# A projection's PSUM bank, one sum instead of two, and softmax reciprocals on GpSimd in a decoder layer

## The chip, the cores and the metric

The kernel runs on one core of a Trainium2 chip. The metric is the device time of one execution in microseconds, as the median of several runs. TensorE is called PE below (its weight loads PEld), VectorE is DVE, ScalarE is ACT, GpSimd is POOL, and SP is the queue that issues most DMAs.

## The reference, cut to what matters

One decoder layer on 512 tokens of width 1024, all in float32:

```python
h = rmsnorm(x, g_mix_pre)
z = h @ w_in                       # columns of four head groups
ya = short_conv_mixer(a_in, a_c, a_b, conv_w)
yb = pool_mixer(pv, pool_w, pool_scale)
yc = dsa_mixer(...)                # 4 heads, each query keeps its 128 best-scored keys
yd = moba_mixer(...)               # 4 heads, causal softmax
mix = concat([ya, yb, yc, yd]) @ w_out
x = x + rmsnorm(mix, g_mix_post)
f = swiglu(rmsnorm(x, g_ffn_pre), w_gate_up, w_down)
x = x + rmsnorm(f, g_ffn_post)
x = x + sigmoid(rmsnorm(x, g_ple) @ w_ple_gate) * (p @ w_ple_proj)
```

The softmax of both attention mixers divides every row of exponentials by its sum. `rmsnorm` scales each token by the reciprocal root of the mean of its squares.

## The kernel before, in words

**Layout.** Activations stand with the features on the 128 partitions and the 512 tokens along the free dimension, so a vector of 1024 features is eight tiles. Every operand of a projection is split into a high and a low part, and a product is three matmuls (`mm3`, L188 to L190): high by high, high by low, low by high. Weights arrive in pieces in the order of `PLAN`; `get` (L180) sees to it that the piece two places ahead is split, the high part by ACT (L169), the low part by DVE or POOL (L173), whichever `lo_engine` names.

**Order.** PE's instructions stand in the order in which they are written. The other engines' order in the attention stage is planned when the kernel is built, from the builder's own durations; inside `with tc.manual_schedule()`, as in `boundary`, all engines keep the written order. All engines take their instructions in order. `later` and `tick` put work off by a number of PE steps.

**PSUM.** Eight banks in three rings: `pmm` (four), `pss` (two), `ptt` (two). A new tile of a ring takes the bank of the oldest one, and waits until that has been read.

**Attention.** The values' projection (L551 to L559) fills all four `pmm` banks. ACT and then DVE take each of the four out (L564, L565). Then `attend` (L654) runs 32 units, a head and a block of 128 queries each: first 16 of `moba`, then 16 of `dsa`. Each unit is `logits` (two matmuls into `pss`, DVE's bias and row maximum at L606, ACT's exponential with its row sum in `st[:, 1:2]` at L608), `weights` (the reciprocal of that sum at L612, a multiplication by it on ACT at L613) and, three units later, `transpose` (PE at L627 into `ptt`, ACT at L630, DVE at L631); `values` closes a head. Between these PE runs steps of `fill`: the remaining projections, of which `keep("pv0")` is the first. `helper` (L569) gives POOL the low parts, bias sums and some elementwise work in units below 20, and DVE the same from unit 20 on. The rounds of the top-128 search (L508, L509) are DVE work that goes in between.

**Boundaries.** Two times, after `w_out` and after `w_down`, `boundary` (L846) closes one norm and starts the next projection. Its last operand tile comes from `post(pt, 7, ...)`: ACT's square of it is `sq7`; the squares of the first seven tiles are already summed in `sums`. `Rms.add` multiplies four 128-column blocks by a column of ones, which gives each token's sum on the partitions; `Rms.sums` does this for `sums` and then for `sq7` into the same columns, then DVE scales (L254) and POOL takes the power of -1/2 (L255). `spread` transposes the four columns back into a full tile in a `ptt` bank (L260). While that chain runs, PE does steps of the small `ple` product (24 matmuls in eight steps) through `go`; ACT takes its four results out (L822). After the spread DVE multiplies and adds (L865, L870), ACT and DVE split (L873, L877), and the first matmul at L908 needs tile 0 of that. Of the eight steps, three are ahead of the spread and five behind it.

Of the kernel before, what the change touches and what calls it, by code (L numbers as in the profile page):

```python
# [9 lines left out]
F32 = mybir.dt.float32  # L10
F32R = mybir.dt.float32r
AF = mybir.ActivationFunctionType
OP = mybir.AluOpType
# [3 lines left out]
P = 128  # L17
# [5 lines left out]
NT = T // P  # L23
# [82 lines left out]
def tile_trunk(ctx: ExitStack, tc: tile.TileContext, xT, pT, sm, relx, wts, outT):  # L106
    nc = tc.nc
    G = ctx.enter_context(tc.tile_pool(name="glob", bufs=1))
# [4 lines left out]
    def pmm():  # L113
        return ps.tile([P, T], F32, tag="mm", bufs=4, name="pmm")

    def pss():
        return ps.tile([P, T], F32, tag="s", bufs=2, name="pss")

    def ptt():
        return ps.tile([P, T], F32, tag="tt", bufs=2, name="ptt")  # L120
# [7 lines left out]
    def tick():  # L128
        clock[0] += 1
        due = [p for p in put_off if p[0] <= clock[0]]  # L130
        put_off[:] = [p for p in put_off if p[0] > clock[0]]
        for _, fn, args in due:
            fn(*args)
# [61 lines left out]
    def single(name, act, pt, ks, start=True, stop=True, cw=P):  # L195

        w = get(name)
        for i, k in enumerate(ks):
            mm3(pt[:cw], w, act[k], (slice(None), slice(i * cw, (i + 1) * cw)), ALL,
                start and i == 0, stop and i == len(ks) - 1)  # L200
            if i < len(ks) - 1:
                yield
# [24 lines left out]
    smt = G.tile([P, SMW], F32, name="smt")  # L227
    ones = G.tile([P, 1], F32, name="ones")
    nc.vector.memset(ones, 1.0)
    mhalf = G.tile([P, NT], F32, name="mhalf")  # L230
    nc.vector.memset(mhalf, -0.5)

# [6 lines left out]
    class Rms:  # L239

        def add(self, sq, first, last):
            if first:
                self.pt = pss()
            for j in range(NT):
                nc.tensor.matmul(self.pt[:, j:j + 1], sq[:, j * P:(j + 1) * P], ones, start=first and j == 0,
                                 stop=last and j == NT - 1, skip_group_check=True)

        def sums(self, sq, first=True):  # L250
            self.add(sq, first, True)
            pt = self.pt
            self.r4 = G.tile([P, NT], F32, tag="r4", bufs=2, name="r4")
            nc.vector.tensor_scalar(self.r4, pt[:, :NT], 1.0 / D, 1e-6, OP.mult, OP.add)  # L254
            nc.gpsimd.tensor_tensor(self.r4, self.r4, mhalf, OP.pow)  # L255
# [19 lines left out]
    with tc.tile_pool(name="mix", bufs=1) as M:  # L275
        def tmp(shape=(P, T), name="tmp", dt=F32):
            return M.tile(list(shape), dt, tag="tmp", bufs=8, name=name)
# [298 lines left out]
        class Attn:  # L576
# [32 lines left out]

            def weights(self, it):  # L610
                st, pr = self.st.pop(it), self.pr[it]
                nc.vector.reciprocal(st[:, 2:3], st[:, 1:2])  # L612
                nc.scalar.activation(pr, pr, AF.Copy, scale=st[:, 2:3])  # L613

            def transpose(self, it):
# [69 lines left out]
        plain = {}  # L685

        def keep(name):
            pt = pmm()
            yield from single(name, h, pt, K8)
            z = plain[name] = tmp(name=name)  # L690
            nc.vector.tensor_tensor(z, pt, r1.rb, OP.mult)
            if name[:2] == "pv":
                pool_sums(int(name[2]))
            if name[:3] == "a_b":
                conv_group(int(name[3]))
            yield

        def pool_sums(m):
            v = plain.pop(f"pv{m}")
            s, w = v, 1  # L700
            for lv in range(2 * m + 2):
                rows = slice(64, P) if lv == 2 * m + 1 else slice(0, P)
                t = tmp(name="ws")
                nc.gpsimd.tensor_tensor(t[rows, w:], s[rows, w:], s[rows, :T - w], OP.add)
                nc.gpsimd.tensor_copy(t[rows, :w], s[rows, :w])
                if lv < 2 * m + 1:
                    s, w = t, 2 * w
            fa = _SM["fac"][0] + 16 * m
            for rows, u in ((slice(0, 64), s), (slice(64, P), t)):
                nc.gpsimd.tensor_tensor(u[rows, :16], u[rows, :16], smt[rows, fa:fa + 16], OP.mult)  # L710
                later(16, nc.vector.scalar_tensor_tensor, t[rows], u[rows], col("invw", m)[rows], v[rows], OP.mult,
                      OP.subtract)
            later(17, pool_split, m, t)
# [17 lines left out]
        def conv_group(m):  # L731
            a, c, b = (plain.pop(f"{n}{m}") for n in ("a_in", "a_c", "a_b"))
            eng = helper()
            eng.tensor_tensor(a, a, c, OP.mult)
            eng.tensor_scalar(c, a, col("conv", 3 * m + 2), 1.0, OP.mult, OP.mult)

            def taps():
                for s in (1, 2):
                    nc.vector.scalar_tensor_tensor(c[:, s:], a[:, :T - s], col("conv", 3 * m + 2 - s), c[:, s:],
                                                   OP.mult, OP.add)  # L740
                eng.tensor_tensor(c, c, b, OP.mult)
                y[m] = (yslot("yh"), yslot("yl"))
                later(3, split, y[m][0], y[m][1], c, 1)
            later(4, taps)
# [80 lines left out]
        for n in range(3, 8):  # L825
            pt = pt3 if n == 3 else pmm()
# [16 lines left out]
            if n < 7:  # L843
                post(pt, n, "g_mix_post", mg[n], ss, tmp)

        def boundary(sums, sq7, fill, x, add, gname, hdst, xdst, sqt, name):  # L846


            def go(n):
                for _ in range(n):  # L850
                    if next(fill, 0) == 0:
                        return
                    tick()
            r = Rms()
            r.add(sums, True, False)
            r.sums(sq7, False)
            low2 = convert_high(conv[0])
            go(3)
            r.spread(False)
            xs, hs, sqs = [], [], []  # L860
            ss = G.tile([P, T], F32, tag="ss", bufs=1, name="ss")

            def mul(k):
                if k < KD:
                    nc.vector.tensor_tensor(add[k], add[k], r.rb, OP.mult)  # L865

            def plus(k):
                if k < KD:
                    xn = xdst(k)
                    nc.vector.tensor_tensor(xn, add[k], x[k], OP.add)  # L870
                    xs.append(xn)
                    hs.append((hdst("hhi"), hdst("hlo")))
                    nc.scalar.activation(hs[k][0], xn, AF.Copy, scale=col(gname, k))  # L873

            def low(k):
                if k < KD:
                    nc.vector.scalar_tensor_tensor(hs[k][1], xs[k], col(gname, k), hs[k][0].bitcast(F32),  # L877
                                                   OP.mult, OP.subtract)

            def square(k):  # L880
                sqs.append(ss if k == 0 else sqt(name="sq"))
                nc.scalar.activation(sqs[k], xs[k], AF.Square)

            mul(0)
            plus(0)
            go(1)
            mul(1)
            plus(1)
            low(0)
            mul(2)  # L890
            go(8)
            pts = [pmm() for _ in range(4)]
            for k in K8:
                if k % 2 == 0:
                    w = wparts.pop(f"{name}{k // 2}")
                    send(conv[0] + RAW)
                plus(k + 2)
                low(k + 1)
                mul(k + 3)
                if 0 < k < 5:  # L900
                    square(k - 1)
                if k % 2 == 0 and k > 0:
                    low2 = convert_high(conv[0])
                if k == 0 or k % 2 and k > 1:
                    low2()
                c = [slice(((k % 2) * 4 + n) * P, ((k % 2) * 4 + n + 1) * P) for n in range(4)]
                for n in range(4):
                    nc.tensor.matmul(pts[n], w[0][:, c[n]], hs[k][0], start=k == 0, stop=False)  # L908
                for n in range(4):
                    nc.tensor.matmul(pts[n], w[1][:, c[n]], hs[k][0], start=False, stop=False)  # L910
                for n in range(4):
                    nc.tensor.matmul(pts[n], w[0][:, c[n]], hs[k][1], start=False, stop=k == KD - 1)  # L912
                tick()

            for k in range(1, KD):
                if k + 3 < KD:
                    square(k + 3)
                nc.vector.tensor_tensor(ss, ss, sqs[k], OP.add)
            return xs, hs, pts, ss

        with tc.manual_schedule():
            sq7 = post(pt, 7, "g_mix_post", mg[7], ss, tmp)
# [4 lines left out]
    with tc.tile_pool(name="ffn", bufs=1) as F:  # L927
# [60 lines left out]
        for n in range(KD):  # L988
            pt = pmm()
# [15 lines left out]
        with tc.manual_schedule():  # L1005
            sq7 = post(pt, 7, "g_ffn_post", fg[7], ss, ftmp)
# [22 lines left out]
        for c in (slice(0, 256), slice(256, T)):  # L1029
            pt = pmm()  # L1030
# [70 lines left out]
```

## Time and profile before

| what | value |
|---|---|
| median of 3 runs | 662.59 us (662.24 to 662.73) |
| profiled execution | 662.23 us, span 660.4 us |
| PE busy | 649.7 us, 98% of the span |
| DVE, ACT, POOL busy | 413.5, 283.0, 74.2 us |
| granted TensorE clock | 0.998 of full speed |

Busy time of PE counts pipelined matmuls; for PE, the idle stretches in front of an instruction, with the instruction that ended them, say more than the share. The timeline's columns are: start in us, duration in us, engine, line, operation, output<-inputs, count, and in brackets the idle time before it and what ended it.

### The profile page before, as it was taken

The page shows a single profiled execution, that of the slowest core. Times are in us where ns is not written, and L with a number is a line of the kernel's source. Part 1 is how long each engine was busy: PE and PEld are TensorE (multiplying, and loading weights), DVE is VectorE, ACT ScalarE, POOL GpSimd, SP SyncE. Part 2 cuts the span into 40 slices and gives each one's busy share as a digit, 9 for nine tenths or more (in the row PEclk, how much of TensorE's full clock was granted, in tenths as well). Part 3 has the DMA queues.
Part 4 walks back from the last instruction along what each step waited for, and adds up shares of the span by engine and source line. Part 5 has one row for each costly group of instructions (what it writes and reads, how often), then busy time and mean ns, then how long its engine had stood idle before and what let it go on. Part 6 is the DMA issues. An engine that isn't in the chain of part 4 may idle for free.

```text
span 660.4 us, 8002 instructions
## 1 busy us (share of the span) xinstructions
PE 649.7 (98%) x2993; PEld 533.5 (81%) x2993; DVE 413.5 (63%) x717; ACT 283.0 (43%) x464; POOL 74.2 (11%) x72
## 2 busy tenths in 40 slices
PE   8999999999999999999999999999999999999997
PEld 7887878888777888888888888888888888888886
DVE  6969999998984468665555555555532322243867
ACT  7655255756785555333232323323222322233542
POOL 1112457365021000000000000000000000000000
PEclk9999999999999999999999999999999999999999
DMA  8447522443435513333332332323233323242203
GB/s 311 148 167 229 148 84 94 113 118 89 112 105 202 151 53 96 93 99 95 96 96 95 96 96 97 95 96 96 87 120 104 103 92 107 87 128 65 80 16 127
DMA packets 24774, 74.16 MB, mean 112 GB/s; under 512 B 3522, under 2 KB 3906, under 8 KB 24736
## 3 DMA queue, kind: packets, MB, share of 16 engines
q1 hardware_dynamic: 22656, 67.78, 33.1%
q0 software_dynamic: 2080, 5.88, 2.5%
q8 instruction: 23, 0.38, 0.2%
q14 instruction: 15, 0.12, 0.1%
HBM read 67.20 MB, written 4.74 MB: 109 GB/s over the span
## 4 chain that ended last, share of the span: by engine, by line
PE 78%; DVE 14%; DMA 3%; ACT 2%; issue 2%; SPq 0%; DVEq 0%; ACTq 0%
PE pmm L188 10%; PE pmm L190 9%; PE pmm L189 9%; PE pss L190 7%; PE pss L188 7%; PE pss L189 7%; PE ptt L188 6%; PE ptt L190 6%; PE ptt L189 6%; DVE acc L509 3%; DVE m L508 3%; PE pmm L908 2%; PE pmm L912 2%; PE pmm L910 2%; PE pmm L325 2%
## 5 line engine op out<-in xcount | busy, mean ns | idle before, releaser
L169 ACT ACTIVATE whi<-raw 128x1024 fp32r<-128x1024 f32 (+2 forms) x111 | 113.8, 1025 | 245.0 <-PE pmm L189 82.6
L173 DVE TENSOR_TENSOR wlo<-raw,whi 128x1024 fp32r<-128x1024 f32 (+2 forms) x96 | 112.6, 1173 | 99.7 <-ACT whi L169 99.6
L188 PE MATMUL pss<-hhi,whi 128*128 128x512 f32 (+1 forms) x184 | 72.0, 391 | 0.0
L190 PE MATMUL pss<-hhi,wlo 128*128 128x512 f32 (+1 forms) x184 | 71.7, 390 | 0.0
L189 PE MATMUL pss<-hlo,whi 128*128 128x512 f32 (+1 forms) x184 | 71.6, 389 | 0.0
L188 PE MATMUL pmm<-gth,whi 128*128 128x512 f32 x176 | 69.3, 394 | 0.0
L190 PE MATMUL pmm<-gth,wlo 128*128 128x512 f32 x176 | 69.0, 392 | 0.0
L189 PE MATMUL pmm<-gtl,whi 128*128 128x512 f32 x176 | 68.3, 388 | 0.0
L188 PE MATMUL ptt<-hhi,whi 128*128 128x512 f32 x168 | 65.6, 390 | 0.0
L190 PE MATMUL ptt<-hhi,wlo 128*128 128x512 f32 x168 | 65.4, 389 | 0.0
L189 PE MATMUL ptt<-hlo,whi 128*128 128x512 f32 x168 | 65.4, 389 | 0.0
L188 PE MATMUL pmm<-hhi,whi 128*128 128x512 f32 (+1 forms) x144 | 56.8, 395 | 1.3 <-DVE v L565 1.3
L189 PE MATMUL pmm<-hlo,whi 128*128 128x512 f32 (+1 forms) x144 | 54.8, 381 | 0.0
L190 PE MATMUL pmm<-hhi,wlo 128*128 128x512 f32 (+1 forms) x144 | 54.7, 380 | 0.0
L965 DVE TENSOR_TENSOR us<-ptt,rb 128x512 f32<-128x512 f32 x19 | 13.1, 692 | 48.7 <-PE ptt L190 48.7
L173 POOL TENSOR_TENSOR wlo<-raw,whi 128x1024 fp32r<-128x1024 f32 x15 | 36.1, 2408 | 40.8 <-ACT whi L169 38.2
L190 PEld LDWEIGHTS pss<-hhi,wlo 128*128 128x128 f32 (+1 forms) x184 | 34.2, 186 | 7.6
L189 PEld LDWEIGHTS pss<-hlo,whi 128*128 128x128 f32 (+1 forms) x184 | 34.2, 186 | 7.4
L188 PEld LDWEIGHTS pss<-hhi,whi 128*128 128x128 f32 (+1 forms) x184 | 34.1, 185 | 7.3
L190 PEld LDWEIGHTS pmm<-gth,wlo 128*128 128x128 f32 x176 | 33.0, 188 | 7.7
L189 PEld LDWEIGHTS pmm<-gtl,whi 128*128 128x128 f32 x176 | 33.0, 188 | 7.4
L188 PEld LDWEIGHTS pmm<-gth,whi 128*128 128x128 f32 x176 | 33.1, 188 | 6.6
(270 smaller groups left out, 1191.2 us busy)
## 6 DMA issues: line engine op xcount, KB each, us to landing
raw<-in_wts_dram SPq DMA_DIRECT2D x98, 512.0 KB, 3.5
raw<-in_wts_dram SPq DMA_DIRECT2D x12, 384.0 KB, 3.0
vec_d<-vec POOLq DMA_DIRECT2D x1, 2560.0 KB, 20.5
xb<-in_xT_dram SPq DMA_DIRECT2D x8, 256.5 KB, 6.1
bm<-vec_d SPq DMA_DIRECT2D x8, 256.0 KB, 2.8
xr<-in_xT_dram POOLq DMA_DIRECT2D x8, 256.0 KB, 5.9
out_dram<-th SPq DMA_DIRECT2D x7, 256.0 KB, 2.0
klow<-klow SPq DMA_DIRECT2D x8, 128.0 KB, 2.9
```

What stands on the lines that cost most here:

```text
L169: nc.scalar.activation(hi, src, AF.Copy)
L173: lo_engine[0].tensor_tensor(lo, src, hi.bitcast(F32), OP.subtract)
L188: nc.tensor.matmul(out, a[0][sa], b[0][sb], start=start, stop=False)
L189: nc.tensor.matmul(out, a[0][sa], b[1][sb], start=False, stop=False)
L190: nc.tensor.matmul(out, a[1][sa], b[0][sb], start=False, stop=stop)
L325: nc.tensor.matmul(pts[n][:, P:], w[a][:, c[n]], h[k][b][:, P:], start=k + a + b == 0, stop=k == 7 and b == 1)
L508: nc.vector.max(m8, acc[i])
L509: nc.vector.match_replace(out=acc[i], in_to_replace=m8, in_values=acc[i], imm_value=TAKEN)
L908: nc.tensor.matmul(pts[n], w[0][:, c[n]], hs[k][0], start=k == 0, stop=False)
L910: nc.tensor.matmul(pts[n], w[1][:, c[n]], hs[k][0], start=False, stop=False)
L912: nc.tensor.matmul(pts[n], w[0][:, c[n]], hs[k][1], start=False, stop=k == KD - 1)
L965: nc.vector.tensor_tensor(us, pu, rb, OP.mult)
```

## The change

A column of -1 is set once. The reciprocal of each softmax sum is taken by POOL as the power of -1 instead of by DVE's reciprocal. The first kept projection, `pv0`, takes a `ptt` bank and not a `pmm` bank. In `boundary`, DVE adds `sq7` to `sums` first; the product with ones is done once and not twice; two `ple` steps go ahead of it and two more ahead of the spread.

```diff
+    minus = G.tile([P, 1], F32, name="minus")
+    nc.vector.memset(minus, -1.0)
...
-        def add(self, sq, first, last):
-            if first:
-                self.pt = pss()
+        def sums(self, sq):
+            pt = pss()
             for j in range(NT):
-                nc.tensor.matmul(self.pt[:, j:j + 1], sq[:, j * P:(j + 1) * P], ones, start=first and j == 0,
-                                 stop=last and j == NT - 1, skip_group_check=True)
-
-        def sums(self, sq, first=True):
-            self.add(sq, first, True)
-            pt = self.pt
+                nc.tensor.matmul(pt[:, j:j + 1], sq[:, j * P:(j + 1) * P], ones, start=j == 0, stop=j == NT - 1,
+                                 skip_group_check=True)
...
             def weights(self, it):
                 st, pr = self.st.pop(it), self.pr[it]
-                nc.vector.reciprocal(st[:, 2:3], st[:, 1:2])
+                nc.gpsimd.tensor_tensor(st[:, 2:3], st[:, 1:2], minus, OP.pow)
                 nc.scalar.activation(pr, pr, AF.Copy, scale=st[:, 2:3])
...
         def keep(name):
-            pt = pmm()
+            pt = ptt() if name == "pv0" else pmm()
...
             r = Rms()
-            r.add(sums, True, False)
-            r.sums(sq7, False)
+            nc.vector.tensor_tensor(sums, sums, sq7, OP.add)
+            go(2)
+            r.sums(sums)
             low2 = convert_high(conv[0])
-            go(3)
+            go(2)
             r.spread(False)
```

## Rows read from the trace of the kernel before

**Rows 1.** The page's busy time of engines over the whole span.
```profile
PE 649.7 (98%) x2993; PEld 533.5 (81%) x2993; DVE 413.5 (63%) x717; ACT 283.0 (43%) x464; POOL 74.2 (11%) x72
```
**Rows 2.** Windows: stretch, us, then busy us (count) of PE, PEld, DVE, ACT, POOL.
```profile
90.00:160.00 70.00, 69.95 (x344) 57.42 (x344) 68.93 (x173) 43.71 (x97) 41.66 (x35) 1.00 0.35 100
170.00:190.00 20.00, 18.22 (x97) 14.33 (x97) 19.92 (x55) 15.28 (x39) 0.00 (x0) 1.00 0.22 63
```
**Rows 3.** Timeline of PE, 170 to 190 us, where it sat idle.
```profile
171.66 0.38 PE L433 MATMUL pss<-ck,cq 128*128 128x256 f32 x1 [0.40 <-DVE st L606]
173.74 0.44 PE L627 MATMUL ptt<-smt,pr 128*128 128x128 f32 x2 [0.87 <-DVE pt L631]
183.68 0.41 PE L627 MATMUL ptt<-smt,pr 128*128 128x128 f32 x2 [0.51 <-DVE pt L631]
```
**Rows 4.** Timeline from the first logits to the first matmul of pv0.
```profile
85.57 0.28 PE L434 MATMUL pss<-klow,dq 128*128 128x256 f32 x1
...
86.40 0.73 DVE L565 SCALAR_TENSOR_TENSOR v<-pmm,r,v 128x512 fp32r<-128x512 f32 x1
...
87.19 0.50 PE L188 MATMUL pmm<-hhi,whi 128*128 128x512 f32 x1 [1.34 <-DVE v L565]
```
**Rows 5.** Timeline of the first boundary, from its sums to the next projection.
```profile
232.27 0.95 PE L247 MATMUL pss<-ones,ss 128*128 128x1 f32 x8
232.47 0.60 ACT L798 ACTIVATE sq<-pmm 128x512 f32<-128x512 f32 x1 [3.62 <-PE pmm L190]
...
233.12 1.05 PE L247 MATMUL pss<-ones,sq 128*128 128x1 f32 x8
...
234.03 0.48 PE L188 MATMUL pmm<-pp,klow 128*128 128x512 f32 x1
...
234.46 1.05 POOL L255 TENSOR_TENSOR r<-r,mhalf 128x4 f32<-128x4 f32 x1 [32.88 <-DVE r L254]
...
235.99 0.59 PEld L260 LDWEIGHTS ptt<-smt,r 128*128 128x128 f32 x4
...
238.31 0.72 ACT L873 ACTIVATE hhi<-x,smt 128x512 fp32r<-128x512 f32 x1 [1.98 <-DVE x L870]
...
240.16 1.23 PE L908 MATMUL pmm<-hhi,whi 128*128 128x512 f32 x4
...
240.89 0.19 PEld L908 LDWEIGHTS pmm<-hhi,whi 128*128 128x128 f32 x1 [0.31 <-ACT pph L822]
```
**Rows 6.** The chain that ended last: the second boundary's sums on it.
```profile
602.17 1.74 PE pss L247 x16
```
**Rows 7.** Groups by line: count, then busy us and mean ns of one, then idle before.
```profile
L612 DVE RECIPROCAL st<-st 128x1 f32<-128x1 f32 x32 | 4.8, 152 | 1.3 <-ACT pr L608 1.2
L255 POOL TENSOR_TENSOR r<-r,mhalf 128x4 f32<-128x4 f32 x5 | 6.0, 1196 | 245.2 <-DVE r L254 245.2
L705 POOL COPY ws<-ws 128x2 f32<-128x2 f32 x1 | 0.2, 184 | 0.0
L800 DVE TENSOR_TENSOR ss<-ss,sq 128x512 f32<-128x512 f32 x12 | 8.2, 685 | 6.1 <-ACT sq L798 6.1
L415 DVE TENSOR_TENSOR z<-z,dq 128x512 fp32r<-128x512 f32 x2 | 1.4, 679 | 0.0
```
**Rows 8.** Timeline of DVE: one reciprocal and the instruction behind it.
```profile
120.62 0.15 DVE L612 RECIPROCAL st<-st 128x1 f32<-128x1 f32 x1
120.70 0.07 DVE L509 MATCH_VALUE_LOAD acc<-m,acc 128x8 f32 x1
```
**Rows 9.** Waits over the whole span: ACT's for the reciprocals (us, times, longest).
```profile
ACT pr L613 <- DVE st L612: 13.1, 14, 3.4
```
**Rows 10.** Timeline: a POOL instruction and a DVE instruction of two SBUF inputs beside it.
```profile
157.00 2.40 POOL L173 TENSOR_TENSOR wlo<-raw,whi 128x1024 fp32r<-128x1024 f32 x1 [0.24 <-ACT whi L169]
...
157.48 2.48 DVE L415 TENSOR_TENSOR z<-z,cq 128x512 fp32r<-128x512 f32 x1 [0.52 <-ACT cq L414]
```
**Rows 11.** Timeline of DVE ahead of the second boundary: the last split of its `ple` operands.
```profile
594.60 0.68 DVE L223 TENSOR_TENSOR pp<-praw,pp 128x512 fp32r<-128x512 f32 x1
```

## The prediction, made before the changed kernel was run

> **What bounds the kernel now.** I read the page first: PE is busy for 649.7 of 660.4 us [rows 1]. So only two things shorten the kernel: PE work that goes away, and the few stretches in which PE sits idle. Next I read the list of PE's waits, and looked each one up in the timeline. Four matter here. PE waits 1.34 us ahead of the first matmul of `pv0`, because its `pmm` bank is the one from which DVE is still taking the values [rows 4]. It waits 0.40, 0.87 and 0.51 us between 170 and 190 us, each time for DVE [rows 3]; that is 1.8 us. The windows say why: DVE is full in both parts of the attention stage, 68.9 of 70 us and 19.9 of 20 us, while POOL is busy for 41.7 of the first 70 us and for none of the other 20, and ACT has 26 us to spare in the first part and 5 in the second [rows 2]. From 90 to 160 us PE nevertheless runs without a gap, since DVE's top-128 rounds fill its idle time and stand behind the urgent work. Last I read the two boundaries in the timeline. There PE has no gap to speak of, but it does sums that could be done once: 16 passes in 1.74 us at the second boundary [rows 6], and at the first the passes over `sums` from 232.27 us and those over `sq7` from 233.12 to 234.03 us [rows 5].
>
> **The bank of pv0.** In a `ptt` bank the first matmul need not wait for DVE. The ring is free then: the first transposes come three units later, when `pv0` has been taken out, and need one bank at a time. The next `pmm` tile is `pv1`'s, 24 matmuls later, and by then the values are out. Its split weights were made two pieces ahead. So PE is 1.34 us ahead from there [rows 4]. It keeps the lead as far as 170 us, because there is no PE wait before that.
>
> **The reciprocals.** DVE loses 32 instructions of 0.15 us, 4.8 us in all [rows 7]. As the next instruction starts 0.08 us after a reciprocal [rows 8], what DVE really gains is between 32 x 0.08 = 2.6 us and 4.8 us, plus the 1.2 us in which it stood idle for ACT ahead of two of them [rows 7]. Some seven of the 32 lie between 170 and 190 us: 0.6 to 1.1 us there. POOL gains 32 powers of 128x1. The trace has none; the nearest rows are the power of 128x4, 1.05 us [rows 5], and a copy of 128x2, 0.18 us [rows 7]. I take 0.4 us, an estimate: the copy's 0.18 plus a quarter of the remaining 0.87, for one column of four. The bounds are 0.18 and 1.05. That is 13 us of POOL time (6 to 34). Behind the waiting power on POOL stand low parts of weights, made two pieces ahead, and bias sums, one unit ahead; behind the waiting multiplication on ACT stand other units' exponentials and high parts. ACT already waits 13.1 us in 14 of 32 places for the reciprocal [rows 9], since DVE's queue is full; where POOL is idle, from unit 20 on, the wait should shrink.
>
> What can go against it is the port. A DVE instruction with two SBUF inputs took 2.48 us when it met a POOL instruction of 2.40 us [rows 10], against 0.68 us for the same line alone [rows 7]; it ended 0.56 us after POOL did, so it stood still until POOL was done. With a power of 0.4 us in each 3.3 us, about one such DVE instruction in eight is met, for 0.2 us on average: some 40 of them, by the list of groups, make 1 us, inside the 2.6 us gained. With 1.05 us nearly one in three is met, for half a microsecond: 7 us, more than is gained. I take the small value, as in size the new power is nearest to the copy. The Trainium skill (SBUF — State Buffer, Who interferes with whom) says the same as these two rows, that the pair of ports DVE shares with GpSimd is locked for a whole instruction, when DVE has two SBUF inputs and GpSimd reads; by that rule alone the reciprocal, with one input, was better off on DVE.
>
> Between 170 and 190 us I therefore leave the 1.8 us of waits nearly as they are: PE comes 1.34 us earlier, ACT and DVE, which follow PE, come earlier too by most of that, and DVE has 0.6 us less to do there. I count 0.1 us. The bounds are a gain of all 1.8 us and a loss of the whole 1.34 us. Attention: 1.4 us gained.
>
> **The boundaries.** Eight passes go: 0.91 us, from 233.12 to 234.03 [rows 5]. Moved ahead of the sums are six matmuls. Nine take 1.96 us, from 234.03 to 235.99 [rows 5], so 0.22 us each, and six last from 232.27 to about 233.6. Meanwhile the square ends at 233.07 and the new DVE add takes 0.68 us [rows 5, 7]; with the 0.05 us from ACT's end to PE's start seen there, the sums start at 233.84. PE waits about 0.25 us. The eight passes then end at 234.75. POOL's power started 1.34 us after the passes over `sq7` [rows 5], so now at 235.18, and ends at 236.23; the spread can load at 236.28, where it loaded at 235.99. PE has finished its next six matmuls by 236.05: a second wait of some 0.25 us. From the spread to L908 it was 240.16 - 235.99 = 4.17 us; three matmuls fewer stand there now (0.68 us), so L908 starts at 236.28 + 3.49 = 239.77. Tile 0, ready 3.04 us after the spread's load [rows 5], is there at 239.3 and makes no new wait. The fourth weight load no longer waits 0.31 us for ACT's copy of the second `ple` result [rows 5], which now comes ahead of tile 1; PE's four matmuls lost some 0.15 us to that. Sum: 0.4 + 0.15, rounded down to 0.5 us at a boundary, 1.0 us for both. Without either wait it would be 2.1 us; with 0.15 us more on each hand-over 0.4 us. The `ple` operands are needed 1.8 us sooner; their last split ends at 595.3 us in the second boundary [rows 11], some 7 us ahead of that. The DMA that `get` issues moves with them on a queue that has nothing late. The new memset is one small DVE instruction at the start, beside the first loads: nothing.
>
> **Sum.** 1.4 + 1.0 = 2.4 us off a span of 660.4. The profiled execution took 662.23 us, so 659.8; the median of the runs is 0.36 us above it, which gives **660.2 us**.
>
> **Rivals.** (a) *The lead is given back.* DVE is full from 170 us on and gets no freer, because the powers hold its two-input instructions as in [rows 10]; the waits of [rows 3] grow by 1.34 us. For it: 19.9 of 20 us busy [rows 2]. Against it: POOL has nothing else to do there. Only the boundaries are left: 662.6 - 1.0 = 661.6 us, no change that can be told. The same rule of the skill would make this so.
> (b) *The relief counts in full.* The waits of [rows 3] go too: 1.34 + 1.8 + 1.0 = 4.1 us, 658.5 us. For it: the gain of 2.6 us or more exceeds them. Against: most of it falls where PE does not wait.
> (c) *POOL's queue is the new wait, and it is slower.* Place: units 0 to 19, where POOL is busy 60% of the time, mostly with low parts of 2.4 us [rows 2, 10]. A power of 1.05 us behind 0.6 x 1.2 = 0.7 us of other work and 0.14 us of hand-overs costs ACT 1.9 us a unit, against 0.4 now (13.1/32) [rows 9]: 20 x 1.5 = 30 us, where ACT has 26 to spare [rows 2]. The missing 4 us reach PE through late transposes: 662.6 - 2.4 + 4 = 664.2 us. It decides once a unit costs ACT 1.3 us more than now. Against it: three units lie between the exponential and its transposes, and a power of 0.4 us leaves it far from that.
>
> **How the numbers follow.** A measurement here can tell 0.2%, or 1.3 us, from no change: faster means under 661.3, slower over 663.9. The forecast has 0.60, (b) 0.12, (a) 0.20, (c) 0.08. So faster 0.72, same 0.20, slower 0.08. By the bounds of its terms the forecast's own range is 659.0 to 661.2. The range of 658.4 to 662.4 takes in (a) with the boundaries at their low end and (b) at its price, and leaves out (c) and the better half of (b).
>
> **What would show it.** PE's 1.34 us at `pv0` gone; eight passes of L247 at each boundary, and L908 starting 0.4 us sooner after the last matmul of `w_out`; POOL's power at about 0.4 us; PE's waits from 170 to 190 us at 1.5 to 2 us. The prediction is wrong if these waits double, if PE waits for transposes below unit 20, or if a power takes a microsecond and ACT's waits for it pass 30 us.

## The result, and the profile after

The changed kernel takes 667.43 us (median; 667.02 to 668.89), the kernel before 662.41 us in the same session: a ratio of 1.0078 (95% interval 1.0066 to 1.0090), so 5 us slower. 660.2 us was forecast, and the range ended at 662.4. The profiled execution of the changed kernel took 668.89 us, 1.5 us over its own median, so amounts below come from medians where there are any.

The page's busy line of the changed kernel, beside [rows 1]:

```profile
PE 651.4 (98%) x2977; PEld 531.3 (80%) x2977; DVE 417.6 (63%) x688; ACT 283.0 (42%) x464; POOL 95.8 (14%) x104
```

PE has 16 matmuls less and DVE 29 instructions less (32 reciprocals gone, two additions and a memset new). By their durations that should make DVE 3.4 us less busy (4.8 less, 1.4 more). It is busy 4.1 us more: about 7.5 us have gone into instructions that were there before.

PE's waits for DVE and ACT in the attention stage and at the late sums, from the list of waits of the changed kernel (total us, times, longest):

```profile
PE ptt L624 <- DVE pt L628: 5.1, 6, 2.5
...
PE pss L430 <- ACT rl L492: 1.2, 2, 1.0
PE pss L430 <- DVE st L603: 1.0, 1, 1.0
PE pmm L188 <- DVE ol L648: 0.9, 1, 0.9
PE pss L248 <- DVE ss L916: 0.4, 1, 0.4
```

The 1.34 us ahead of `pv0` [rows 4] are gone. But PE now waits 5.1 us for transposes' banks, which DVE's low part of the softmax weights (`pt`) leaves late, and 0.9 us ahead of a pool mixer's product, which by this list waits for the `pmm` bank that DVE reads out for `ol`. Its longest wait is 2.5 us, at 146.93 us. The timeline of the changed kernel there:

```profile
141.52 1.60 DVE L736 SCALAR_TENSOR_TENSOR a_c<-a_in,smt,a_c 128x511 f32<-128x511 f32 x1
...
142.65 0.88 POOL L609 TENSOR_TENSOR st<-st,minus 128x1 f32<-128x1 f32 x1
...
143.51 2.35 POOL L173 TENSOR_TENSOR wlo<-raw,whi 128x1024 fp32r<-128x1024 f32 x1
143.65 2.76 DVE L736 SCALAR_TENSOR_TENSOR a_c<-a_in,smt,a_c 128x510 f32<-128x510 f32 x1
146.33 0.55 DVE L628 TENSOR_TENSOR pt<-ptt,pt 128x384 fp32r<-128x384 f32 x1
...
146.93 0.33 PE L624 MATMUL ptt<-smt,pr 128*128 128x128 f32 x1 [2.50 <-DVE pt L628]
```

And of the kernel before, the same work:

```profile
137.39 1.67 DVE L739 SCALAR_TENSOR_TENSOR a_c<-a_in,smt,a_c 128x511 f32<-128x511 f32 x1
...
139.05 0.67 DVE L509 MATCH_REPLACE8 acc<-m,acc 128x512 f32<-128x512 f32 x1
...
139.71 0.53 DVE L631 TENSOR_TENSOR pt<-ptt,pt 128x384 fp32r<-128x384 f32 x1
140.17 2.07 DVE L739 SCALAR_TENSOR_TENSOR a_c<-a_in,smt,a_c 128x510 f32<-128x510 f32 x1
```

Before, `pt` stood between the two taps of the convolution. Now it stands behind both, and the second tap, which starts with a POOL low part of 2.35 us, takes 2.76 us. The power in these lines ends before that tap starts, so it does not hold the tap; the low part follows it on POOL without a gap. What moved is **the order in which DVE does its other work**. That order is planned when the kernel is built. In the traces of the attention stage (from 55 us on), without the reciprocals, at least 38 of DVE's 308 instructions have to be moved to get from the old order to the new one. ACT's order has changed too, by 28 of 188.

The powers themselves, as a group (least, median and longest ns; first and last start), and who waited for them:

```profile
L609 POOL TENSOR_TENSOR st<-st,minus x32: 539/560/1030, 91.1 to 200.3; 128x1 f32<-128x1 f32 x32
...
  ACT pr L610: 11.8, 15
```

A power takes 0.55 us alone and up to 1.03 us. ACT waits 11.8 us for them in 15 places, where it waited 13.1 us in 14 for DVE's reciprocals [rows 9]: that hand-over got no dearer.

The windows of the changed kernel, the first two beside [rows 2] (they hold somewhat earlier work than there, since all is later); the clock is the third column from the end:

```profile
90.00:160.00 70.00, 65.61 (x319) 52.57 (x318) 68.37 (x153) 41.03 (x92) 48.24 (x51) 1.00 0.33 95
170.00:190.00 20.00, 18.02 (x83) 13.68 (x82) 17.32 (x41) 13.97 (x33) 5.35 (x7) 0.91 0.39 98
...
178.00:180.00 2.00, 1.13 (x6) 0.71 (x6) 2.00 (x7) 1.14 (x2) 0.64 (x1) 0.81 0.65 175
180.00:182.00 2.00, 2.00 (x9) 1.81 (x8) 2.00 (x7) 1.59 (x6) 1.57 (x2) 0.50 0.08 32
```

PE sat idle for 4.4 us of the first 70. In the second part DVE has 2.7 us of idle time, where it had 0.1, and PE waits all the same.

At the boundaries the change did what it should. The timeline of the first one after the change, beside [rows 5]:

```profile
239.99 0.69 DVE L852 TENSOR_TENSOR ss<-ss,sq 128x512 f32<-128x512 f32 x1 [3.47 <-ACT sq L795]
240.74 0.97 PEld L248 LDWEIGHTS pss<-ones,ss 128*128 128x128 f32 x8 [0.45 <-DVE ss L852]
...
242.08 1.04 POOL L252 TENSOR_TENSOR r<-r,mhalf 128x4 f32<-128x4 f32 x1 [33.49 <-DVE r L251]
...
243.17 0.41 PEld L257 LDWEIGHTS ptt<-smt,r 128*128 128x128 f32 x4 [0.33 <-POOL r L252]
```

The two waits (0.45 and 0.33 us, forecast 0.25 each) and eight passes instead of 16 are there.

I laid PE's matmuls of both traces side by side and took, for each, the later start minus the earlier one. Where that difference jumps, time was lost or won: -1.6 us at `pv0`; then +0.6, +0.4, +1.2 (the pool mixer), +0.6, +2.7 (the place shown above), +0.7 up to 177 us, +1.5 at the low clock and +0.3 at 190 us; -0.7 and -0.5 at the boundaries; +1.0 at the late sums near 642 us. Another 0.9 us lies ahead of the attention stage, where nothing was changed.

### The profile page after: what moved, and what is told of

Its sections match the earlier page's. It is cut to its first block, busy times and chain, and to the rows that moved or that the text cites. A ratio compares the mean times of both kernels' runs of the same rounds, so it can differ in the third digit from the quotient of the medians.

```text
span 667.1 us, 7988 instructions
## 1 busy us (share of the span) xinstructions
PE 651.4 (98%) x2977; PEld 531.3 (80%) x2977; DVE 417.6 (63%) x688; ACT 283.0 (42%) x464; POOL 95.8 (14%) x104
## 4 chain that ended last, share of the span: by engine, by line
PE 76%; DVE 15%; DMA 3%; ACT 2%; issue 2%; SPq 0%; POOL 0%; ACTq 0%; DVEq 0%; POOLq 0%
PE pmm L188 9%; PE pmm L190 9%; PE pmm L189 9%; PE pss L188 7%; PE pss L190 7%; PE pss L189 7%; PE ptt L188 6%; PE ptt L189 6%; PE ptt L190 6%; DVE acc L506 4%; DVE m L505 3%; PE pmm L906 2%; PE pmm L910 2%; PE pmm L908 2%; PE pmm L322 2%
## 5 line engine op out<-in xcount | busy, mean ns | idle before, releaser
L188 PE MATMUL ptt<-hhi,whi 128*128 128x512 f32 x176 | 68.7, 390 | 0.0
L189 PE MATMUL ptt<-hlo,whi 128*128 128x512 f32 x176 | 68.5, 389 | 0.0
L190 PE MATMUL ptt<-hhi,wlo 128*128 128x512 f32 x176 | 68.5, 389 | 0.0
L188 PE MATMUL pmm<-hhi,whi 128*128 128x512 f32 (+1 forms) x136 | 53.9, 396 | 0.0
L189 PE MATMUL pmm<-hlo,whi 128*128 128x512 f32 (+1 forms) x136 | 51.9, 382 | 0.0
L190 PE MATMUL pmm<-hhi,wlo 128*128 128x512 f32 (+1 forms) x136 | 51.7, 380 | 0.0
L963 DVE TENSOR_TENSOR us<-ptt,rb 128x512 f32<-128x512 f32 x19 | 13.1, 692 | 48.9 <-PE ptt L190 48.9
L252 POOL TENSOR_TENSOR r<-r,mhalf 128x4 f32<-128x4 f32 x5 | 6.0, 1195 | 245.0 <-DVE r L251 245.0
```

The costliest lines, as they stand in the source:

```text
L188: nc.tensor.matmul(out, a[0][sa], b[0][sb], start=start, stop=False)
L189: nc.tensor.matmul(out, a[0][sa], b[1][sb], start=False, stop=False)
L190: nc.tensor.matmul(out, a[1][sa], b[0][sb], start=False, stop=stop)
L963: nc.vector.tensor_tensor(us, pu, rb, OP.mult)
```

## The experiments

Medians, and ratios against runs of the kernel before on the same chip. Three chips were used; the median of the kernel before was 662.71 us beside e1 to e4, 662.56 beside e5, e6, e7 and e9, and 662.54 beside the others. Costs and gains below are against these, unless two runs are named.

| label | what | median us | ratio (95%) |
|---|---|---|---|
| e1_no_pow | the change, reciprocals on DVE | 662.08 | 0.9991 (0.9982 to 1.0001) |
| e2_pow_alone | only the powers on POOL | 667.45 | 1.0073 (1.0058 to 1.0088) |
| e3_bank_alone | only `pv0`'s bank | 662.51 | 0.9997 (0.9988 to 1.0006) |
| e4_sums_alone | only the boundaries | 662.16 | 0.9990 (0.9981 to 1.0000) |
| e5_pow_unused | powers on POOL that nobody reads | 663.00 | 1.0009 (1.0000 to 1.0019) |
| e6_copy | a copy on POOL in the power's place | 664.19 (663.60 to 667.23) | 1.0036 (1.0021 to 1.0050) |
| e7_pow_from20 | powers from unit 20 on | 663.68 | 1.0016 (1.0007 to 1.0025) |
| e8_pow_to20 | powers in units 0 to 19 | 666.69 | 1.0061 (1.0047 to 1.0075) |
| e9_pow_order | e2, one order forced | 665.84 | 1.0048 (1.0032 to 1.0065) |
| e15_no_division | e1 without reciprocals | 664.46 | 1.0028 (1.0017 to 1.0040) |
| e14_one_tap | e1 with one tap less | 660.50 | 0.9968 (0.9956 to 0.9980) |
| e10_sums_later | e1, late sums a step later | 661.07 | 0.9978 (0.9969 to 0.9987) |

### Which part costs: e1 to e4

Each takes one or two of the three edits; e1 for example

```diff
-                nc.gpsimd.tensor_tensor(st[:, 2:3], st[:, 1:2], minus, OP.pow)
+                nc.vector.reciprocal(st[:, 2:3], st[:, 1:2])
```

> The whole change except that DVE keeps the reciprocals. Theory A, that the powers on POOL cost the time (DVE's two-input instructions held longer, ACT's multiplication and DVE's transposes later): PE keeps the 1.4 us it gains at pv0 and the boundaries give 0.5 to 0.7 us each, so 660 us or a little above, 2 us under the kernel before. Theory B, that the new order of PE's work (pv0 in the transposes' ring, PE earlier than DVE) makes PE wait for the transposes: 665 us or more, as in the changed kernel.

> The kernel before with the powers on POOL alone. Theory A: PE waits 5 to 6 us for transposes between 100 and 190 us, against 1.4 us before, and the time is 666 to 669 us. Theory B: at most 1 us from the kernel before, 662 to 663.5 us.

> The kernel before with pv0 in a ptt bank alone. Theory A: the 1.34 us wait at pv0 is gone and at least half of it is kept, 661 to 662 us. Theory B: waits for transposes below unit 20 appear, 664 us or more.

> The kernel before with the single sums alone. Both theories: 0.75 us and 0.6 us less at the two boundaries, as the changed kernel's trace shows, less the wait of 0.4 us for the last add of squares that stands behind the second one: 661.3 to 661.9 us.

The powers alone cost 4.7 us of the 5.0, as theory A said of e2; the rest of the change is worth -0.6 us (e1), which can't be told from nothing. So e1 lies between its theories: the powers are the cost, but the lead of `pv0` is not kept. e3 fits neither of its theories, and e4 is 0.3 us above its range. DVE's order in the attention stage is that of before in e1, e3 and e4 (at most one instruction moved); that of e2 is the changed kernel's, but for one. The list of waits of e2 has what the changed kernel has, with `pv0`'s wait still there:

```profile
PE ptt L629 <- DVE pt L633: 4.8, 4, 2.5
PE pmm L188 <- DVE v L567: 1.4, 1, 1.4
```

The bank alone wins 1.6 us and gives it back by 145 us (0.9 and 0.6 us), in two waits that the kernel before does not have. The timeline of e3:

```profile
114.47 0.44 PE L627 MATMUL ptt<-smt,pr 128*128 128x128 f32 x2 [0.72 <-DVE pt L631]
...
144.56 0.38 PE L433 MATMUL pss<-ck,cq 128*128 128x256 f32 x1 [0.61 <-DVE st L606]
```

Here DVE's order is the one of before. From 102 us on DVE has hardly a gap and goes through the same list at its own pace, so what PE is ahead it waits for later.

The boundaries alone win 0.7 and 0.5 us of PE's place and give back 1.0 us in this trace, most of it at the next norm's sums, near 636 us, where PE waits 0.41 us. Timeline there, first the kernel before, then e1, whose DVE work at this place is e4's:

```profile
629.02 4.53 DVE L918 TENSOR_TENSOR ss<-ss,sq 128x512 f32<-128x512 f32 x6
633.47 1.22 DVE L173 TENSOR_TENSOR wlo<-raw,whi 128x1024 fp32r<-128x1024 f32 x1
634.60 0.69 DVE L918 TENSOR_TENSOR ss<-ss,sq 128x512 f32<-128x512 f32 x1
...
636.15 0.94 PE L247 MATMUL pss<-ones,ss 128*128 128x1 f32 x8
```

```profile
627.77 2.94 DVE L916 TENSOR_TENSOR ss<-ss,sq 128x512 f32<-128x512 f32 x4
632.23 1.23 DVE L173 TENSOR_TENSOR wlo<-raw,whi 128x1024 fp32r<-128x1024 f32 x1 [1.52 <-ACT whi L169]
633.37 2.14 DVE L916 TENSOR_TENSOR ss<-ss,sq 128x512 f32<-128x512 f32 x3
...
635.66 1.02 PE L248 MATMUL pss<-ones,ss 128*128 128x1 f32 x8 [0.41 <-DVE ss L916]
```

The low part stood behind six of the seven additions; now it stands behind four, and DVE idles 1.52 us for its high part with three additions queued behind. A place in DVE's order again.

### Time on POOL, or order: e5 to e9

e5 keeps DVE's reciprocals, which ACT reads, and adds 32 powers:

```diff
                 nc.vector.reciprocal(st[:, 2:3], st[:, 1:2])
+                sp = M.tile([P, 1], F32, tag="sp", bufs=6, name="sp")
+                nc.gpsimd.tensor_tensor(sp, st[:, 1:2], minus, OP.pow)
```

e6 puts `nc.gpsimd.tensor_copy(st[:, 2:3], st[:, 1:2])` where e2 has the power; e7 and e8 choose by `slot[0] >= 20` and `slot[0] < 20` between the power and DVE's reciprocal. e9 is e2 with the two taps of the first convolution group put behind `pt` of the third moba head's third block (`lows` keeps the DVE instruction of each block):

```diff
-                for s in (1, 2):
-                    nc.vector.scalar_tensor_tensor(c[:, s:], a[:, :T - s], ...
+                with tc.issue_after(lows[(2, 2)]) if m == 0 else ExitStack():
+                    for s in (1, 2):
+                        nc.vector.scalar_tensor_tensor(c[:, s:], a[:, :T - s], ...
...
-            later(4, taps)
+            later(8 if m == 0 else 4, taps)
```

> The kernel before, DVE keeps the reciprocals, and POOL takes the 32 powers as well, into a column that nobody reads. Theory P, that POOL's own time and the port it shares with DVE cost the 4.8 us: 666 us or more, nearly as with the powers in use. Theory O, that the wait of ACT for POOL moves DVE's planned order, so that parts of the transposes stand behind instructions that are held: 662 to 663.5 us.

> The powers of the kernel with the powers alone replaced by a copy of the sum on POOL (the division by the softmax sum is left out, the weights are scaled by the sum). Theory P: a copy takes 0.2 us where a power takes 0.55 to 1.0, so the loss falls from 4.8 us to about 1.5 us, 664 us. Theory O: ACT still waits for POOL, the order stays as with the powers, 666 us or more.

> The kernel before with POOL's powers only from unit 20 on, DVE's reciprocals below that. Both theories: POOL does nothing else from unit 20 on, the steps of 2.7 us and 0.6 us in the trace lie below it, so 662 to 663.2 us. If the loss comes from ACT's wait itself, wherever it is: 664 us or more.

> The kernel before, with the powers on POOL in units 0 to 19 alone. With powers from unit 20 on alone the kernel was 1.1 us slower, with all 32 of them 4.9 us. Theory T (the two halves of the stage are paid separately): 3.8 us, so 666.3 us. Rival U (the order of the first half is worth less by itself, the later units make it worse): under 665 us.

> The kernel with the powers alone, with one order forced on DVE: the conv taps of group 0 are issued behind the low part of the transposes of unit 10, where the kernel before has one ahead and one behind. Theory O: the step of 2.7 us at PE's transposes of unit 12 goes, and with it the clock's half speed after it, 664 us or less. Theory P: the held time comes back at another instruction, 666 us or more.

The powers' own time on POOL, with whatever they hold up on DVE, costs 0.4 us (e5), as theory O said. POOL's busy time rises there by 22 us, as in the change, so this is not what costs 4.7.

A copy in their place, with the result still going through POOL, costs 1.6 us (e6). That is theory P's number, and O's 666 us is missed. But O's premise does not hold either: the order does not stay as with the powers, 19 of DVE's 308 instructions stand elsewhere than in e2. So e6 doesn't decide between time and order. Its ten times reach from 663.6 to 667.2 us, for a reason that is not known, and its profiled execution was 3 us over its median, so its trace is not used for amounts.

e8 measured 4.1 us against 3.8 expected (the expectation's 4.9 us for all 32 powers took e2 against another chip), e7 1.1 us, between its two values: the two halves are paid about separately, and some four fifths of the loss are in units 0 to 19, where POOL has its long low parts.

Forcing one place of DVE's order (5 of 308 instructions moved against e2) gives back some 1.5 of e2's 4.7 us. That lies between O's value and P's, and both have a part in it. The two taps, 1.60 and 2.76 us in e2 as in the changed kernel, take 0.74 and 1.17 us in e9's timeline, and e2's wait of 2.5 us at 146.31 us is gone. But a wait of 0.98 us for `st`, at 174.69 us, is new (0.19 us in e2); the longest wait for `pt`, 1.2 us near 187 us, is in e2 as well. Timeline and list of waits of e9:

```profile
142.91 0.74 DVE L744 SCALAR_TENSOR_TENSOR a_c<-a_in,smt,a_c 128x511 f32<-128x511 f32 x1
...
145.31 1.17 DVE L744 SCALAR_TENSOR_TENSOR a_c<-a_in,smt,a_c 128x510 f32<-128x510 f32 x1
```

```profile
PE ptt L629 <- DVE pt L633: 2.6, 4, 1.2
```

### DVE relieved, with nothing put on POOL: e15

ACT multiplies by the sum itself.

```diff
-                nc.vector.reciprocal(st[:, 2:3], st[:, 1:2])
-                nc.scalar.activation(pr, pr, AF.Copy, scale=st[:, 2:3])
+                nc.scalar.activation(pr, pr, AF.Copy, scale=st[:, 1:2])
```

> The change with no reciprocals at all: ACT multiplies by the sum itself (the softmax division is left out), so DVE is relieved of 32 instructions and POOL gets none. This prices the relief alone. Theory D (DVE's amount of work gives back the lead): the lead of 1.4 us is kept and some of the 1.8 us of waits from 170 to 190 us goes, 659.0 to 660.8 us. Rival N (the places in the planned order decide): 661.5 to 663 us, with the order of DVE changed and PE waiting elsewhere.

This is the relief that the change is about, at no price on any other engine, and it makes e1 **2.4 us slower** (664.46 against 662.08, on two chips with nearly the same kernel before). Theory D's gain did not come; N's mechanism did, at a higher price than N's 663 us. Its page shows the first sign in one line:

```profile
PE 648.4 (98%) x2977; PEld 530.9 (80%) x2977; DVE 415.2 (63%) x688; ACT 282.6 (43%) x464; POOL 73.6 (11%) x72
```

With 32 instructions less than e1, DVE is as busy as there (415.0 us): what the reciprocals took has gone into others. PE's two waits at 113.70 and 143.79 us in e1, 0.67 and 0.68 us, are 1.58 and 1.84 us long in e15. Timeline of e1 at the first of them, then of e15 at both:

```profile
112.23 0.75 DVE L223 TENSOR_TENSOR pw<-smt,pw 128x128 fp32r<-128x128 f32 x1
...
112.98 0.67 DVE L628 TENSOR_TENSOR pt<-ptt,pt 128x512 fp32r<-128x512 f32 x1
...
113.70 0.44 PE L624 MATMUL ptt<-smt,pr 128*128 128x128 f32 x2 [0.67 <-DVE pt L628]
```

```profile
112.91 1.35 DVE L223 TENSOR_TENSOR pw<-smt,pw 128x128 fp32r<-128x128 f32 x1
114.18 0.08 DVE L506 MATCH_VALUE_LOAD acc<-m,acc 128x8 f32 x1
114.25 0.67 DVE L506 MATCH_REPLACE8 acc<-m,acc 128x512 f32<-128x512 f32 x1
114.85 0.68 DVE L627 TENSOR_TENSOR pt<-ptt,pt 128x512 fp32r<-128x512 f32 x1
...
115.58 0.44 PE L623 MATMUL ptt<-smt,pr 128*128 128x128 f32 x2 [1.58 <-DVE pt L627]
...
142.48 2.60 DVE L735 SCALAR_TENSOR_TENSOR a_c<-a_in,smt,a_c 128x510 f32<-128x510 f32 x1
...
145.07 0.67 DVE L506 MATCH_REPLACE8 acc<-m,acc 128x512 f32<-128x512 f32 x1
145.66 0.68 DVE L687 TENSOR_TENSOR a_b<-pmm,rb 128x512 f32<-128x512 f32 x1
146.26 0.54 DVE L603 CUSTOM_DVE_ANT_0 pr<-pss,bm 128x384 f32<-128x384 f32 x1
...
146.87 0.39 PE L430 MATMUL pss<-ck,cq 128*128 128x256 f32 x1 [1.84 <-DVE st L603]
```

Two things are to be seen. A top-128 round (`MATCH_REPLACE8`) stands ahead of `pt` and of the row maximum for which PE waits, so the rounds are not always behind the urgent work; nor were they in the kernel before, where one at 139.05 us stands ahead of `pt` at 139.71 us (timeline above). And the split of `pw` takes 1.35 us and the tap 2.60 us, where the kernel before has 0.75 and 2.07 us for the same instructions: shifted, they meet more of POOL's old work. The sum of what DVE instructions over 0.2 us longer than the shortest of their kind lose between 90 and 200 us is 7.1 us before, 7.0 us in e1, 10.1 us in e15 and 11.5 us in the changed kernel (six to eight instructions each). At least 35 of DVE's 308 instructions stand elsewhere than before in e15, much the same moves as in the changed kernel (14 differ between these two); of ACT's 188, 29.

e6, whose results all go through POOL, has nearly the order of e15, where none does (9 of 308 differ), and costs about as much. So the route through POOL by itself seems cheap; no run tests it in a kept order. e15 and e6 work on other numbers than the kernel, since the division is left out; that this leaves the times alone is not shown.

### What DVE's amount of work is worth in a kept order: e14

```diff
-                for s in (1, 2):
+                for s in ((1, 2) if m > 0 else (1,)):
```

> The change with DVE's reciprocals, and the second tap of the first convolution group left out (part of the convolution is not computed), 2.07 us less of DVE work near 141 us. Theory D (DVE is full from 102 to 160 us and so its work gives back the lead that pv0's bank brings): the PE wait of 0.6 us near 144 us goes and that part of the lead is kept, about 661.5 us. Rival N (PE's waits come from single instructions that stand late in DVE's planned order, whatever it has to do in all): the wait appears at another place, 662.1 us.

660.50 us, 1.6 us less than e1 (1.4 us when each is taken against the kernel before on its own chip), for 2.07 us of DVE work. Only three of DVE's instructions stand elsewhere than in e1. So in an order that is otherwise kept, DVE's work does set PE's place, as theory D says, and by more than the one wait that it named: PE's waits for `st` fell from 1.1 us (e10, below, alike in this stage) to 0.2 us.

### The rest of the change, mended: e10

```diff
-        rb, steps = late_norm(single("pg_n4", h3, p4, K8), lambda: single("pg_n5", h3, p5, K8), ss, 6, 2)
+        rb, steps = late_norm(single("pg_n4", h3, p4, K8), lambda: single("pg_n5", h3, p5, K8), ss, 7, 2)
```

> The change with DVE's reciprocals, and the late norm's sums behind seven steps of PE and not six. Theory S (the gain at the second boundary is partly given back at these sums, because DVE's add behind them is not done when PE comes, 0.41 us of wait in the same kernel with six steps; one step of 0.7 us more covers it): no PE wait for ss there, 0.5 us less than that kernel's 662.1, so 661.6 us, ratio to the kernel before 0.9985. Rival E (the end is set by the chain behind the norm, not by PE's place): the spread or the output tiles come later by the same step, 662.1 us.

661.07 us, 1.0 us less than e1 and 1.5 us less than the kernel before: this version beats the kernel before, by 0.2%, and the interval of its ratio ends below 1. The sums no longer wait (timeline of e10; no bracket behind the row):

```profile
635.85 0.95 PE L248 MATMUL pss<-ones,ss 128*128 128x1 f32 x8
```

E falls. Each against the kernel before on its own chip, the gain over e1 is 0.8 us, against 0.5 us expected; 0.4 us is the wait, the rest lies within the intervals of the two medians.

## Why the prediction was wrong

**The step that failed** is the price of the reciprocals' move. The prediction counted 2.6 us or more of relief on DVE and 1 us of holding by the powers, both on a DVE order that it took as given, "since DVE's top-128 rounds fill its idle time and stand behind the urgent work". The order is not given: the kernel's description says that it is planned from the builder's durations, but no term and no rival asked what the plan does when 32 instructions leave it. e15 prices that alone: +2.4 us against e1, without a single power. With the powers it is some 5.4 us (667.43 against e1's 662.08). If the parts add, 3.0 us are left: the powers' own time and holding (0.4 us in e5, whose order differs from the one before by 18 of 308), the 14 further moves, the route to ACT through POOL, and the lower clock told of at the end. How they divide stays open: an order forced at more places than e9's one was not tried, nor the old order with powers whose results are used.

**The holding** was the right mechanism on the wrong instructions. The prediction looked for DVE instructions met by the new powers, about one in eight. What grew was the time lost to POOL's old work, from 7.1 to 11.5 us, and of that from 4.8 to 9.6 us beside low parts of 2.4 us, through instructions that now start beside one. Of the eight held ones in the changed kernel each ends 0.5 to 0.6 us after an old POOL instruction, none after a power. The rule cited from the Trainium skill (SBUF — State Buffer, Who interferes with whom) agrees with this trace: the 2.76 us tap started 0.14 us into a POOL low part of 2.35 us and ended 0.55 us after it; a two-input instruction of that width takes 0.68 us alone [rows 7].

**The power** took 0.55 us alone and 0.70 us on average (22.2 us for 32), against 0.4 us estimated and bounds of 0.18 and 1.05.

**The bank of pv0.** 1.34 us were forecast and 1.6 us came (e3), but "it keeps the lead as far as 170 us, because there is no PE wait before that" was wrong: a list of waits shows where PE is late, not how little it is from being late. DVE busy for 68.9 of 70 us [rows 2] was the sign. That is rival (a)'s outcome, from 114 us on and not from 170 us, and without its mechanism, since e3 has no powers; its 661.6 us is near e1's 662.08.

**The boundaries** were right in their steps: 0.7 and 0.5 us (e4) against 0.5 each, with both waits a little longer than worked out. Missing was what came later: PE, ahead, met the next norm's additions, in a changed order there too, and lost 1.0 us there.

**Rivals.** (c) ended on the right side by a mechanism that did not happen: ACT's waits for POOL fell to 11.8 us. (b) is refuted by e15: with the relief in full, the kernel is slower. Of the prediction's own signs of being wrong one came true: PE waits for transposes below unit 20, 3.4 us up to 147 us. Its waits from 170 to 190 us stayed at 1.85 us.

## What to carry to other kernels

Where an engine's order is planned from durations, an edit that only takes work away from it is an edit of its whole order: compare the order of the engines before and after, and price the change with the work simply left out. An engine without a gap over tens of microseconds can take back the lead that PE wins there, as in e3, even if PE shows no wait; so look for the relief that leaves the order alone (e14) or win time behind that stretch (e10). Long GpSimd instructions are best kept from starting beside VectorE's two-input ones, and after every reordering those meetings are to be counted anew.

## What was not expected of the hardware

In the profiled execution of the changed kernel PE was busy for only 1.1 of 2 us between 178 and 180 us; its granted clock fell to 0.81 in that window and to 0.50, the lower level of 1.2 GHz, in the next, where PE was busy all the time (windows above). That cost about 1.5 us of PE's place in this trace. The trace of the kernel before shows 1.00 from 170 to 190 us [rows 2]. The traces of e2, e7 and e8 have such a stretch too, each in or right behind one or two PE waits of 0.8 to 2.5 us; it cost 1.1 to 1.4 us there. The window of e2 behind its wait of 2.5 us:

```profile
146.00:148.00 2.00, 1.69 (x5) 1.40 (x6) 2.00 (x7) 0.00 (x0) 1.07 (x1) 0.50 0.65 197
```

So a PE wait can cost more than its length, and part of what the powers cost in these traces is the clock. Not every long wait is followed by this: e15 waits 1.84 us at 146.87 us, and its clock reads 1.00 from 144 to 148 us. In the trace of e9, where the wait of 2.5 us is gone, the clock stays at 1.00 there as well. Of the runs that were only timed just the mean clock is on record: 0.997 to 0.999 in those of the changed kernel, 0.996 to 0.999 in e2 and e8, 0.998 to 1.000 in those of the kernel before beside the experiments.
